# A Trainium2 trunk kernel: the state-space scans of half 0, two octets in one chain of operations

## The chip, the cores and the metric

The kernel runs on one core of one Trainium2 chip. The metric is device time in microseconds of one launch, as the median of several runs. Five engines work side by side, each on its own list of instructions in order: TensorE (PE: matmuls, into PSUM banks), VectorE (DVE), ScalarE (ACT), GpSimd (POOL) and SyncE (SP: here it only issues DMAs). They meet through semaphores. SBUF is the working memory; PSUM is the small memory that TensorE writes and that VectorE and ScalarE read and write.

## The reference, cut to what matters

One layer over 2048 positions of width 1024: a diagonal complex state-space mixer (S5), a gated linear unit behind it, a squared-ReLU MLP, a gated embedding and RMS norms. The change is in the mixer's scan:

```
bu_re = einsum('blgh,gph->blgp', ug, bb_re)      # 64 groups, 64 complex states each
bu_im = einsum('blgh,gph->blgp', ug, bb_im)
def combine(left, right):                        # x[l] = a * x[l-1] + bu[l], complex
    a1r, a1i, b1r, b1i = left
    a2r, a2i, b2r, b2i = right
    return (a2r*a1r - a2i*a1i, a2r*a1i + a2i*a1r,
            a2r*b1r - a2i*b1i + b2r, a2r*b1i + a2i*b1r + b2i)
_, _, xs_re, xs_im = associative_scan(combine, (a_re, a_im, bu_re, bu_im), axis=1)
y = einsum(xs_re, c_re) - einsum(xs_im, c_im)
```

## The kernel before, in words

The sequence is cut into two halves of 1024 positions, each half into 128 chunks of 8 positions. Inside a chunk the mixer is a product with small matrices that are made from powers of the decay; across the chunks a scan over 128 chunk states remains. The 64 groups form 8 octets of 8 groups; an octet's chunk states are a tile `xs` of 128 partitions (two groups' 64 states) by 2 (real, imaginary) by 4 by 128 chunks. The change concerns half 0, where octets are taken in four pairs (pair 0 to pair 3). Half 1 is scanned octet by octet later, from SBUF, between matmuls of the gated linear unit.

For an octet of half 0, `sums` (L595) has TensorE put the chunk sums into `xs`, a PSUM tile of its own from the pool `ps_x` with two buffers. `scan` (L613) then works on `xs` in place on VectorE: 7 levels up and 6 down, 13 in all, each with one multiplication by powers of the decay (`tm<-al,xs`) and two additions (`xs<-xs,tm`), every one dependent on the one before. `together` (L716) takes one operation of the pair's first octet, then one of its second, and so on, and starts other work of the plan at given steps. After that `stack` (L661) copies the result out of PSUM: on ScalarE, the first octet's copies and its `carry`, then the second's (in the last pair VectorE does the second's). Then TensorE makes the sums of the next pair's first octet, VectorE (or POOL) the matrices `vm` of that octet (`make_v`), then come the second octet's sums. The order on each engine is written out by hand there; the code order is the engine order. The low parts `al_y` of the mixer's output are made on VectorE inside the scans (`low`), after ScalarE has made the high parts `ah_y`.

At the start, `turned` (L244) turns the matrices b and c through TensorE into PSUM; four of its eight results use `ps_x` buffers, the other four other pools. In that part a scheduler sets the order on all engines but ScalarE. `al` (L124) holds the powers of the decay for all octets, `amul` (L618) forms a product with them, and the buffer `tm` (L854) has two copies in half 0.

Of the kernel before, what the change touches and what calls it, by code (L numbers as in the profile page):

```python
# [9 lines left out]
F32 = mybir.dt.float32  # L10
# [14 lines left out]
C = 128  # L25
# [5 lines left out]
NOCT = 8  # L31
# [7 lines left out]
def trunk(  # L39
# [31 lines left out]
    def tt(o, a, b, op):  # L71
        return dve.tensor_tensor(out=o, in0=a, in1=b, op=op)  # L72

    def mul(o, a, b):
        return tt(o, a, b, ALU.mult)
# [19 lines left out]
    const = ctx.enter_context(tc.tile_pool(name="const", bufs=1))  # L95
# [4 lines left out]
    ps_s5 = banks0.enter_context(tc.tile_pool(name="ps_s5", bufs=2, space=PSUM))  # L100

    sums0 = ExitStack()
    ps_x = sums0.enter_context(tc.tile_pool(name="ps_x", bufs=2, space=PSUM))
    ps_mm = None

    edge = ctx.enter_context(tc.tile_pool(name="edge", bufs=1, side="right"))
# [14 lines left out]

    ident = const.tile([P, P], F32, name="ident")
    make_identity(nc, ident)
    al = const.tile([P, 8, NOCT, 2, 2, 4], F32, name="al")  # L124
    carry = const.tile([P, 2, 32], F32, name="carry")
    dve.memset(carry, 0.0)
    g_ffn = const.tile([P, KT], F32, name="g_ffn")
# [85 lines left out]
    sp.dma_start(out=gn[:, 0], in_=norm_ffn[0].rearrange("(k q) -> k q", q=P))  # L213
    sp.dma_start(out=gn[:, 1], in_=norm_ple[0].rearrange("(k q) -> k q", q=P))
    xs0 = stat_loads(0)
    sq = small.tile([P, 2, NOCT, 4], F32, name="sq", bufs=1)
    sgn = sq[:, 0, 0, 0:1]
    pool.memset(sgn[0:S], 1.0)
    pool.memset(sgn[S:P], -1.0)
# [21 lines left out]
    y1 = par.tile([P, G, H], F32, name="y1")  # L241
    y2 = par.tile([P, G, H], F32, name="y2")

    def turned(above, below, hh, nm, pool_=None, tag="s5"):  # L244

        if pool_ is None:
            ps = ps_x.tile([P, 2, 8, G], F32, tag="x", name=f"bc_{nm}_{hh}")[:, 0]
        else:
            ps = pool_.tile([P, 8, G], F32, tag=tag, name=f"bc_{nm}_{hh}")
        for h in range(8):  # L250
            for half, src in enumerate((above, below)):
                if half:
                    pe.matmul(ps[S:P, h], src(hh * 8 + h), ident[0:G, 0:G], start=True, stop=True)  # L253
                else:
                    pe.transpose(out=ps[0:S, h], in_=src(hh * 8 + h), identity=ident[0:G, 0:G])
        return ps[:, :].rearrange("p h g -> p g h")
# [165 lines left out]

    for e in range(2):
        ls = slice(e * S, e * S + S)
        pr = pw_r[ls, 8].rearrange("p (o i e) -> p e o i", e=2, i=4)[:, e]
        pi = pw_i[ls, 8].rearrange("p (o i e) -> p e o i", e=2, i=4)[:, e]
        for r_ in range(2):
            dve.tensor_copy(out=al[ls, 0, :, 0, r_], in_=pr)
            ts(al[ls, 0, :, 1, r_], pi, 1.0 - 2 * r_, ALU.mult)

    def decay_steps():
        for k in range(7):
            re, im = al[:, k, :, 0, 0], al[:, k, :, 1, 0]
            mul(sq[:, 0], re, re)
            yield
            mul(sq[:, 1], im, im)
            yield
            ri = al[:, k + 1, :, 1, 1]
            mul(ri, re, im)
            yield  # L440
            tt(al[:, k + 1, :, 0], sq[:, 0].unsqueeze(2).broadcast_to([P, NOCT, 2, 4]),
               sq[:, 1].unsqueeze(2).broadcast_to([P, NOCT, 2, 4]), ALU.subtract)
            yield
            for r_ in range(2):
                ts(al[:, k + 1, :, 1, r_], ri, 2.0 - 4 * r_, ALU.mult)
                yield
# [18 lines left out]
    class Octet:  # L465
# [129 lines left out]
        def sums(self):  # L595

            if self.hb == 0:
                self.xs = ps_x.tile([P, 2, 4, C], F32, tag="x", name=f"xs_{self.nm}")
                for i in range(4):
                    for c in range(2):  # L600
                        for e in range(2):
                            pe.matmul(self.xs[e * S:(e + 1) * S, c, i], self.wm[:, 2 * i + e, c * S:(c + 1) * S],
                                      self.u[:, 2 * i + e], start=True, stop=True)
                return
            self.xs = self.tile("xs", (P, 2, 4, C))
            for e in range(2):
                ps = ps_s5.tile([P, 4, C], F32, tag="s5", name=f"s{e}_{self.nm}")
                for i in range(4):
                    pe.matmul(out=ps[:, i], lhsT=self.wm[:, 2 * i + e], rhs=self.u[:, 2 * i + e], start=True, stop=True)
                for c in range(2):  # L610
                    act.copy(self.xs[e * S:(e + 1) * S, c], ps[c * S:(c + 1) * S])

        def scan(self):  # L613

            xs, o, i0 = self.xs, self.o, 4 * self.o
            tm = self.tile("tm", (P, 16 * (C // 2)))

            def amul(k, src, n):  # L618
                t_ = tm[:, :16 * n].rearrange("p (a n) -> p a n", n=n)
                a_ = al[:, k, o].rearrange("p a r i -> p (a r i)").unsqueeze(2).broadcast_to([P, 16, n])  # L620
                s_ = src.rearrange("p r i c -> p (r i) c").unsqueeze(1).broadcast_to([P, 2, 8, n])
                mul(t_, a_, s_)
                t4 = tm[:, :16 * n].rearrange("p (a r i n) -> p a r i n", a=2, r=2, i=4)
                return t4[:, 0], t4[:, 1, ::-1]

            for k in range(6 if self.hb else 7):
                l = 1 << k
                t1, t2 = amul(k, xs[:, :, :, l - 1::2 * l], C // (2 * l))
                yield
                dst = xs[:, :, :, 2 * l - 1::2 * l]  # L630
                add(dst, dst, t1)
                yield
                add(dst, dst, t2)
                yield
            cr = carry[:, :, i0:i0 + 4].unsqueeze(3)
            if self.hb == 0:

                for k in range(5, -1, -1):
                    l = 1 << k
                    t1, t2 = amul(k, xs[:, :, :, 2 * l - 1:C - 1:2 * l], C // (2 * l) - 1)  # L640
                    yield
                    dst = xs[:, :, :, 3 * l - 1::2 * l]
                    add(dst, dst, t1)
                    yield
                    add(dst, dst, t2)
                    yield
                return
            self.es = es = self.tile("es", (P, 2, 4, C))
            e0 = es[:, :, :, 0:1]
            pool.tensor_copy(out=e0, in_=cr)  # L650
            for k in range(6, -1, -1):
                l = 1 << k
                t1, t2 = amul(k, es[:, :, :, 0::2 * l], C // (2 * l))
                yield
                dst = es[:, :, :, l::2 * l]
                add(dst, t1, xs[:, :, :, l - 1::2 * l])
                yield
                add(dst, dst, t2)
                yield
# [191 lines left out]

    EB = 3
    sp0 = s5.enter_context(tc.tile_pool(name="s5p", bufs=1, side="right"))
    nb0 = dict(u=4, vm=4, dd0=2, dd1=2, gm=3, tm=2)  # L854
    NP = NOCT // 2


# [24 lines left out]
    with tc.manual_schedule(engines=MANUAL):  # L882
# [94 lines left out]
        for k in range(NP):  # L977
            a, b = 2 * k, 2 * k + 1
            plan = PLAN0 if k == 0 else PLAN1 if k < NP - 1 else PLAN2
            at = [(n, lambda k=k, w=w, i=i: do(k, w, i)) for n, acts in plan for w, i in acts]  # L980
            together((q.scan() for q in pairs[k]), *at)
            octs[a].stack()
            octs[b].stack(k == NP - 1)
            if k < NP - 1:
# [603 lines left out]
```

## Time and profile before

| | |
|---|---|
| median of 3 runs | 2162.16 us (2161.92 to 2165.72) |
| the profiled execution | 2161.0 us, its span 2159.2 us |
| busy, share of the span | PE 94%, DVE 64%, ACT 41%, POOL 19% |
| the chain that ended last, by engine | PE 77%, DVE 12%, issue 3%, ACT 3%, POOL 3%, DMA 2% |
| mean granted TensorE clock | 0.984 |

Times in the rows are microseconds from the span's start. A timeline row merges like instructions that follow one another: start of the first, time from there to the end of the last, engine, line, operation, tile written <- tiles read, shapes, count; in brackets the idle time before it and what ended it. Operations overlap at their ends, so what an operation costs in a row of many is the distance between starts, not its own duration. DVE helpers all have one line (L72), so tiles tell which is which.

### The profile page before, as it was taken

To read this page: it belongs to the slowest core of one execution; us is meant where nothing else is said; L and a number is where in the kernel's file an instruction comes from. 1 tells how busy PE (TensorE), PEld (TensorE's weight loads), DVE (VectorE), ACT (ScalarE), POOL (GpSimd) and SP (SyncE) were. 2 spreads that over 40 slices of the span, in tenths; PEclk is the share of its full clock that TensorE was granted. 3 is DMA by queue.
4 is the path that set the end of the run, shared out by engine and by line. 5 is a ranking of instruction groups with operands and counts; after the bars stand their busy time and mean duration, and the time that the engine had idled before them with its cause. 6 is when DMAs were issued, how large, how long until landed. Compare 5 with 4: busy or idle time off the path is not lost.

```text
span 2159.2 us, 28823 instructions
## 1 busy us (share of the span) xinstructions
PE 2033.9 (94%) x9878; PEld 1680.1 (78%) x9878; DVE 1387.7 (64%) x2614; ACT 886.5 (41%) x1767; POOL 417.6 (19%) x369
## 2 busy tenths in 40 slices
PE   7488999987999999999999999979999999999997
PEld 5477877775788888888887788857888888888876
DVE  5998587766766666876665732367666657555455
ACT  2476354435333235444454521243323355444443
POOL 1575011112322221533210000022222200000000
PEclk9999999998999999999999999989999999999999
DMA  5297644342444449998861631224444498755112
GB/s 167 92 266 204 206 148 124 96 124 70 152 155 156 151 158 347 353 389 305 290 234 67 226 104 40 81 81 144 159 149 148 159 335 294 251 194 191 45 49 88
DMA packets 241957, 377.38 MB, mean 175 GB/s; under 512 B 23681, under 2 KB 106641, under 8 KB 241809
## 3 DMA queue, kind: packets, MB, share of 16 engines
q1 hardware_dynamic: 236880, 360.85, 49.9%
q0 software_dynamic: 4928, 14.69, 2.1%
q8 instruction: 77, 1.26, 0.2%
q14 instruction: 72, 0.58, 0.1%
HBM read 261.21 MB, written 114.23 MB: 174 GB/s over the span
## 4 chain that ended last, share of the span: by engine, by line
PE 77%; DVE 12%; issue 3%; ACT 3%; POOL 3%; DMA 2%; SPq 0%; DVEq 0%; ACTq 0%; POOLq 0%
PE dn L1358 28%; PE up L1266 26%; PE glu L1047 3%; PE glu L1049 3%; PE glu L1048 3%; PE gt L1049 2%; PE gt L1048 2%; PE gt L1047 2%; DVE tm L72 2%; DVE xs L72 2%; DVE es L72 1%; DVE wu L72 1%; ACT xs L668 1%; PE bc_b L253 1%; PE bc_c L253 1%
## 5 line engine op out<-in xcount | busy, mean ns | idle before, releaser
L1266 PE MATMUL up<-h_s,wu 128*128 128x512 f32 x1280 | 407.4, 392 | 6.9 <-DVE ev L72 6.9
L1358 PE MATMUL dn<-h_dw,h_da 128*128 128x512 f32 x896 | 349.1, 390 | 0.0
L1358 PE MATMUL dn<-h_dw,l_da 128*128 128x512 f32 x896 | 348.7, 389 | 0.0
L1358 PE MATMUL dn<-l_dw,h_da 128*128 128x512 f32 x896 | 348.6, 389 | 0.0
L1266 PEld LDWEIGHTS up<-h_s,wu 128*128 128x128 f32 x1280 | 242.4, 189 | 58.9 <-DVE ev L72 8.6
L72 DVE TENSOR_TENSOR l_da<-da,h_da 128x512 fp32r<-128x512 f32 x224 | 178.7, 798 | 168.7 <-ACT h_da L1174 168.6
L1266 PE MATMUL up<-l_s,wu 128*128 128x512 f32 x640 | 250.5, 391 | 0.0
L72 DVE TENSOR_TENSOR wu<-rawu,wu 128x512 fp32r<-128x512 f32 x224 | 164.2, 747 | 114.7 <-ACT wu L1254 114.7
L1174 ACT CAST h_da<-da 128x512 fp32r<-128x512 f32 x224 | 139.1, 621 | 235.8 <-PE dn L1358 211.2
L1047 PE MATMUL glu<-w_glu,ah_y 128*128 128x512 f32 x492 | 195.5, 397 | 5.6 <-ACT w_glu L734 4.7
L1358 PEld LDWEIGHTS dn<-h_dw,l_da 128*128 128x128 f32 x896 | 168.2, 188 | 34.9
L1358 PEld LDWEIGHTS dn<-h_dw,h_da 128*128 128x128 f32 x896 | 168.2, 188 | 34.8
L1358 PEld LDWEIGHTS dn<-l_dw,h_da 128*128 128x128 f32 x896 | 168.2, 188 | 34.7
L1048 PE MATMUL glu<-w_glu,ah_y 128*128 128x512 f32 x492 | 193.5, 394 | 1.3 <-DVE w_glu L72 1.3
L1049 PE MATMUL glu<-w_glu,al_y 128*128 128x512 f32 x492 | 192.6, 392 | 0.0
L1252 POOL TENSOR_TENSOR rawu<-rawu,rawu 128x512 f32<-128x512 f32 x96 | 134.7, 1417 | 298.1 <-DVE wu L72 298.1
L72 DVE TENSOR_TENSOR l_dw<-dw,h_dw 128x512 fp32r<-128x512 f32 x224 | 168.7, 753 | 12.4 <-ACT h_dw L1174 11.0
L1266 PE MATMUL up<-ah_f,wu 128*128 128x512 f32 x512 | 172.4, 398 | 3.5 <-ACT wu L1254 2.8
L1254 ACT CAST wu<-rawu 128x512 fp32r<-128x512 f32 x224 | 131.9, 620 | 91.0 <-POOL rawu L1252 62.2
L1174 ACT CAST h_dw<-dw 128x512 fp32r<-128x512 f32 x224 | 138.1, 617 | 46.1 <-POOL dw L1343 44.4
L1277 ACT COPY ev<-up 128x512 f32<-128x512 f32 x96 | 56.2, 585 | 245.2 <-PE up L1266 245.2
L1266 PEld LDWEIGHTS up<-l_s,wu 128*128 128x128 f32 x640 | 121.2, 189 | 25.2
(312 smaller groups left out, 3398.4 us busy)
## 6 DMA issues: line engine op xcount, KB each, us to landing
da<-h_d SPq DMA_DIRECT2D x224, 256.0 KB, 4.6
dw<-in_mlp_w_dram SPq DMA_DIRECT2D x192, 256.0 KB, 5.1
rawu<-in_mlp_w_dram SPq DMA_DIRECT2D x64, 512.0 KB, 3.8
h_d<-ev SPq DMA_DIRECT2D x96, 256.0 KB, 2.1
h_d<-hs SPq DMA_DIRECT2D x96, 256.0 KB, 2.1
dw<-t_d SPq DMA_DIRECT2D x96, 256.0 KB, 4.4
t_d<-dw SPq DMA_DIRECT2D x64, 256.0 KB, 5.1
raw_glu<-in_ssm_w_glu_dram SPq DMA_DIRECT2D x59, 256.0 KB, 4.0
```

What stands on the lines that cost most here:

```text
L72: return dve.tensor_tensor(out=o, in0=a, in1=b, op=op)
L253: pe.matmul(ps[S:P, h], src(hh * 8 + h), ident[0:G, 0:G], start=True, stop=True)
L668: act.copy(dd[c * S:(c + 1) * S, :, e], self.es[e * S:(e + 1) * S, c])
L1047: pe.matmul(out=ps, lhsT=lh, rhs=rh, start=first, stop=False)
L1048: pe.matmul(out=ps, lhsT=lh, rhs=rl, start=False, stop=False)
L1049: pe.matmul(out=ps, lhsT=ll, rhs=rh, start=False, stop=last)
L1174: act.copy(h_, src)
L1252: pool.tensor_tensor(out=src, in0=src, in1=other, op=ALU.add)
L1254: act.copy(w_[:, 0], src)
L1266: pe.matmul(out=ps, lhsT=lhs, rhs=rhs, start=i in FIRST_IN_CHAIN and k == n == 0, stop=k == 3 and n == 2, skip_group_check=True)
L1277: act.copy(ev[g, i], y_ if i == 5 else x_)
L1358: pe.matmul(out=ps, lhsT=lhs[:, cs_], rhs=rhs, start=i in FIRST_IN_CHAIN and fp == n == 0, stop=fp == NPAIR - 1 and n == 2, skip_group_che ...
```

## The change

In half 0 the sums of a pair's two octets share one PSUM tile of twice the size, `ps_x` has one buffer of that size, and one scan runs on both octets at once: each of its 39 operations is twice as wide, and there is one chain where there were two in turn. `al` is laid out by pairs of octets, so half 1's `amul` takes a slice of it. `turned` takes its four places from one `ps_x` tile. `tm` has one buffer of twice the size.

```
-    ps_x = sums0.enter_context(tc.tile_pool(name="ps_x", bufs=2, space=PSUM))
+    ps_x = sums0.enter_context(tc.tile_pool(name="ps_x", bufs=1, space=PSUM))
-    al = const.tile([P, 8, NOCT, 2, 2, 4], F32, name="al")
+    al = const.tile([P, 8, NOCT // 2, 2, 2, 8], F32, name="al")
...
         if pool_ is None:
-            ps = ps_x.tile([P, 2, 8, G], F32, tag="x", name=f"bc_{nm}_{hh}")[:, 0]
+            if not places:
+                four = ps_x.tile([P, 4, 8, G], F32, tag="x", name=f"bc_{nm}_{hh}")
+                places.extend(four[:, i] for i in range(4))
+            ps = places.pop(0)
...
             if self.hb == 0:
-                self.xs = ps_x.tile([P, 2, 4, C], F32, tag="x", name=f"xs_{self.nm}")
+                if self.o % 2 == 0:
+                    self.both = ps_x.tile([P, 2, 8, C], F32, tag="x", name=f"xs_{self.nm}")
+                else:
+                    self.both = octs[self.o - 1].both
+                self.xs = self.both[:, :, 4 * (self.o % 2):4 * (self.o % 2) + 4]
...
-            xs, o, i0 = self.xs, self.o, 4 * self.o
-            tm = self.tile("tm", (P, 16 * (C // 2)))
+            o, i0 = self.o, 4 * self.o
+            m = 4 if self.hb else 8
+            xs = self.xs if self.hb else self.both
+            tm = self.tile("tm", (P, 4 * m * (C // 2)))
             def amul(k, src, n):
...
+                if self.hb:
+                    a_ = al[:, k, o // 2, :, :, 4 * (o % 2):4 * (o % 2) + 4].unsqueeze(4).broadcast_to([P, 2, 2, m, n])
+                    mul(t_, a_, src.unsqueeze(1).broadcast_to([P, 2, 2, m, n]))
...
-    nb0 = dict(u=4, vm=4, dd0=2, dd1=2, gm=3, tm=2)
+    nb0 = dict(u=4, vm=4, dd0=2, dd1=2, gm=3)
...
-            together((q.scan() for q in pairs[k]), *at)
+            together([pairs[k][0].scan()], *at)
```

VectorE at the first scan (pair 0), before: `tm_0` and `xs_0` are the first octet's, `tm_1` and `xs_1` the second's.

```order
L72 TENSOR_TENSOR tm_0_833<-al,xs_0_730 128x1024 [waits PE_49]
L72 TENSOR_TENSOR tm_1_835<-al,xs_1_760 128x1024 [waits PE_49]
L72 TENSOR_TENSOR xs_0_730<-xs_0_730,tm_0_833 128x512 [waits DVE_49]
L72 TENSOR_TENSOR xs_1_760<-xs_1_760,tm_1_835 128x512 [waits DVE_49]
L72 TENSOR_TENSOR xs_0_730<-xs_0_730,tm_0_833 128x512 [waits DVE_49]
L72 TENSOR_TENSOR xs_1_760<-xs_1_760,tm_1_835 128x512 [waits DVE_49]
L72 TENSOR_TENSOR tm_0_833<-al,xs_0_730 128x512 [waits DVE_49]
L72 TENSOR_TENSOR tm_1_835<-al,xs_1_760 128x512 [waits DVE_49]
```

The same place now:

```order
L72 TENSOR_TENSOR tm_0_829<-al,xs_0_727 128x2048 [waits PE_49]
L72 TENSOR_TENSOR xs_0_727<-xs_0_727,tm_0_829 128x1024 [waits DVE_49] x2
L72 TENSOR_TENSOR tm_0_829<-al,xs_0_727 128x1024 [waits DVE_49]
L72 TENSOR_TENSOR xs_0_727<-xs_0_727,tm_0_829 128x512 [waits DVE_49] x2
L72 TENSOR_TENSOR tm_0_829<-al,xs_0_727 128x512 [waits DVE_49]
L72 TENSOR_TENSOR xs_0_727<-xs_0_727,tm_0_829 128x256 [waits DVE_49] x2
```

Two operations of different octets became one; each waits for the one right before it, where the other octet's operation stood between.

TensorE at the sums of pair 1, before: `xs_2` and `xs_3` are the two octets' tiles, `pp` the work before, `kp` the work behind.

```order
L812 MATMUL pp_1_1_0_1194<-plwh_0_583,plo_1_1_1045 128x512
L602 MATMUL xs_2_1202<-u_2_904,gm_2_603 64x128 [waits DVE_49,Activation_49]
L602 MATMUL xs_2_1202<-u_2_904,gm_2_603 64x128 x15
L602 MATMUL xs_3_1225<-u_3_1069,gm_3_823 64x128 [waits DVE_49,Activation_49]
L602 MATMUL xs_3_1225<-u_3_1069,gm_3_823 64x128 x15
L562 MATMUL kp_2_1260<-y_195,zz 32x16
```

The same place now:

```order
L827 MATMUL pp_1_1_0_1150<-plwh_0_580,plo_1_1_1024 128x512
L611 MATMUL xs_2_1158<-u_2_898,gm_2_600 64x128 [waits DVE_49,Activation_49]
L611 MATMUL xs_2_1158<-u_2_898,gm_2_600 64x128 x15
L611 MATMUL xs_2_1158<-u_3_1048,gm_3_819 64x128 x16
L567 MATMUL kp_2_1215<-y_195,zz 32x16
```

Both octets' sums now write one tile; the one wait left stands at its first matmul, and the second octet's matmuls carry none of their own.

TensorE in the parameter stage, before: `bc_c` are turned parts of c, `tp_small` four small transposes from which ScalarE makes `dm`.

```order
L255 MATMUL bc_c_1_476<-ident,cn_132 64x64
L253 MATMUL bc_c_1_476<-ident,cn_133 64x64
L255 MATMUL bc_c_1_494<-ident,cn_133 64x64
L381 MATMUL tp_small<-ident,dn 128x16
L382 MATMUL tp_small<-ident,dn 128x16
L383 MATMUL tp_small<-ident,gn 128x8
L384 MATMUL tp_small<-ident,gn 128x8
```

The same place now (the turned parts of c are in the tile that is named after b):

```order
L260 MATMUL bc_b_0_197<-ident,cn_132 64x64
L258 MATMUL bc_b_0_197<-ident,cn_133 64x64
L260 MATMUL bc_b_0_197<-ident,cn_132 64x64
L386 MATMUL tp_small<-ident,dn 128x16
L387 MATMUL tp_small<-ident,dn 128x16
L388 MATMUL tp_small<-ident,gn 128x8
L389 MATMUL tp_small<-ident,gn 128x8
```

The small transposes stand 8 matmuls (four steps of two) further ahead, at place 107 of TensorE's list and not at 115; as many matmuls of c follow them.

## Rows read from the trace of the kernel before

**Rows 1.** Windows: stretch, length, busy us (instructions) of PE, PEld, DVE, ACT, POOL; clock; DMA.

```profile
94.00:232.00 138.00, 121.90 (x1066) 104.97 (x1058) 124.82 (x364) 92.86 (x214) 71.98 (x67) 0.96 0.77 214
120.00:122.00 2.00, 1.95 (x18) 1.95 (x20) 1.97 (x2) 1.95 (x6) 2.00 (x2) 0.50 1.09 305
232.00:2159.00 1927.00, 1856.49 (x8512) 1536.76 (x8510) 1195.71 (x2057) 766.98 (x1489) 306.63 (x263) 0.99 0.51 174
```

**Rows 2.** Timeline, VectorE, scan of pair 2: start, duration, line, operation, count, [idle before].

```profile
158.69 2.34 DVE L72 TENSOR_TENSOR tm<-al,xs 128x1024 f32<-128x1024 f32 x2
160.95 2.48 DVE L72 TENSOR_TENSOR xs<-xs,tm 128x512 f32<-128x512 f32 x4
163.34 1.27 DVE L72 TENSOR_TENSOR tm<-al,xs 128x512 f32<-128x512 f32 x2
...
172.12 0.50 DVE L72 TENSOR_TENSOR xs<-xs,tm 128x8 f32<-128x8 f32 x4
172.53 0.30 DVE L72 TENSOR_TENSOR tm<-al,xs 128x16 f32<-128x16 f32 x2
```

**Rows 3.** Timeline, VectorE, the first scan of half 1: one chain of dependent operations.

```profile
261.98 1.23 DVE L72 TENSOR_TENSOR tm<-al,xs 128x1024 f32<-128x1024 f32 x1 [4.03 <-ACT xs L611]
263.25 1.42 DVE L72 TENSOR_TENSOR xs<-xs,tm 128x512 f32<-128x512 f32 x2
264.70 1.07 DVE L72 TENSOR_TENSOR tm<-al,xs 128x512 f32<-128x512 f32 x1
...
271.73 0.18 DVE L72 TENSOR_TENSOR es<-tm,xs 128x8 f32<-128x8 f32 x1
271.94 0.17 DVE L72 TENSOR_TENSOR es<-es,tm 128x8 f32<-128x8 f32 x1
```

**Rows 4.** Timeline, all engines, from the scan of pair 0 to that of pair 1.

```profile
117.27 1.16 ACT L676 COPY dd<-xs 64x508 f32<-64x508 f32 x2 [0.54 <-DVE xs L72]
117.73 1.43 DVE L521 TENSOR_TENSOR vm<-pw_r,y 128x1024 f32<-128x1024 f32 x1
...
120.05 5.19 PE L602 MATMUL xs<-u,gm 128*64 128x128 f32 x64 [2.68 <-ACT carry L677]
...
122.55 0.17 ACT L677 COPY carry<-xs 128x8 f32<-128x8 f32 x1
...
123.54 1.22 DVE L72 TENSOR_TENSOR tm<-al,xs 128x1024 f32<-128x1024 f32 x1
...
126.42 2.49 DVE L72 TENSOR_TENSOR xs<-xs,tm 128x512 f32<-128x512 f32 x4
```

**Rows 5.** Timeline, VectorE and TensorE, the hand-overs to pair 2 and pair 3.

```profile
149.74 3.57 DVE L521 TENSOR_TENSOR vm<-pw_r,y 128x1024 f32<-128x1024 f32 x1
...
155.15 1.97 PE L602 MATMUL xs<-u,gm 128*64 128x128 f32 x32 [0.75 <-ACT carry L677]
...
184.59 1.22 DVE L521 TENSOR_TENSOR vm<-pw_r,y 128x1024 f32<-128x1024 f32 x1
...
195.46 2.49 DVE L72 TENSOR_TENSOR xs<-xs,tm 128x512 f32<-128x512 f32 x4
```

**Rows 6.** Timeline, VectorE and TensorE: waits inside pairs 1 and 3.

```profile
146.17 1.29 DVE L72 TENSOR_TENSOR al_y<-tpy,ah_y 128x512 fp32r<-128x512 f32 x2 [0.74 <-ACT ah_y L741]
...
194.84 0.28 PE L564 MATMUL kp<-vm,zz 128*32 128x112 f32 x1 [0.88 <-POOL vm L524]
...
207.40 1.29 DVE L72 TENSOR_TENSOR al_y<-tpy,ah_y 128x512 fp32r<-128x512 f32 x2 [2.97 <-ACT ah_y L741]
...
214.01 1.29 DVE L72 TENSOR_TENSOR al_y<-tpy,ah_y 128x512 fp32r<-128x512 f32 x2 [3.40 <-ACT ah_y L741]
```

**Rows 7.** Timeline, VectorE and TensorE, the parameter stage at the start.

```profile
47.91 0.17 DVE L72 TENSOR_TENSOR dl<-dm 128x16 f32<-128x16 f32 x1 [14.26 <-ACT dm L388]
...
51.93 0.47 PE L253 MATMUL bc_c<-ident,cn 64*64 64x64 f32 x2
...
53.80 1.22 DVE L521 TENSOR_TENSOR gm<-pw_r,zz 128x1024 f32<-128x1024 f32 x1
```

More of the change, by code (lines that the diff above doesn't have):

```diff
@@ L215, in trunk @@
     xs0 = stat_loads(0)
-    sq = small.tile([P, 2, NOCT, 4], F32, name="sq", bufs=1)
+    sq = small.tile([P, 2, NOCT // 2, 8], F32, name="sq", bufs=1)
     sgn = sq[:, 0, 0, 0:1]
@@ L242, in trunk @@
     y2 = par.tile([P, G, H], F32, name="y2")
+    places = []
     def turned(above, below, hh, nm, pool_=None, tag="s5"):
         if pool_ is None:
-            ps = ps_x.tile([P, 2, 8, G], F32, tag="x", name=f"bc_{nm}_{hh}")[:, 0]
+            if not places:
+                four = ps_x.tile([P, 4, 8, G], F32, tag="x", name=f"bc_{nm}_{hh}")
+                places.extend(four[:, i] for i in range(4))
+            ps = places.pop(0)
         else:
@@ L424, in trunk @@
         ls = slice(e * S, e * S + S)
-        pr = pw_r[ls, 8].rearrange("p (o i e) -> p e o i", e=2, i=4)[:, e]
-        pi = pw_i[ls, 8].rearrange("p (o i e) -> p e o i", e=2, i=4)[:, e]
+        pr = pw_r[ls, 8].rearrange("p (o i e) -> p e o i", e=2, i=8)[:, e]
+        pi = pw_i[ls, 8].rearrange("p (o i e) -> p e o i", e=2, i=8)[:, e]
         for r_ in range(2):
@@ L440, in decay_steps @@
             yield
-            tt(al[:, k + 1, :, 0], sq[:, 0].unsqueeze(2).broadcast_to([P, NOCT, 2, 4]),
-               sq[:, 1].unsqueeze(2).broadcast_to([P, NOCT, 2, 4]), ALU.subtract)
+            tt(al[:, k + 1, :, 0], sq[:, 0].unsqueeze(2).broadcast_to([P, NOCT // 2, 2, 8]),
+               sq[:, 1].unsqueeze(2).broadcast_to([P, NOCT // 2, 2, 8]), ALU.subtract)
             yield
@@ L613, in scan @@
         def scan(self):
-            xs, o, i0 = self.xs, self.o, 4 * self.o
-            tm = self.tile("tm", (P, 16 * (C // 2)))
+            o, i0 = self.o, 4 * self.o
+            m = 4 if self.hb else 8
+            xs = self.xs if self.hb else self.both
+            tm = self.tile("tm", (P, 4 * m * (C // 2)))
             def amul(k, src, n):
[L619 to L624, printed above, removed]
+                t_ = tm[:, :4 * m * n].rearrange("p (a r i n) -> p a r i n", a=2, r=2, i=m)
+                if self.hb:
+                    a_ = al[:, k, o // 2, :, :, 4 * (o % 2):4 * (o % 2) + 4].unsqueeze(4).broadcast_to([P, 2, 2, m, n])
+                    mul(t_, a_, src.unsqueeze(1).broadcast_to([P, 2, 2, m, n]))
+                else:
+                    a_ = al[:, k, o // 2].rearrange("p a r i -> p (a r i)").unsqueeze(2).broadcast_to([P, 4 * m, n])
+                    s_ = src.rearrange("p r i c -> p (r i) c").unsqueeze(1).broadcast_to([P, 2, 2 * m, n])
+                    mul(tm[:, :4 * m * n].rearrange("p (a n) -> p a n", n=n), a_, s_)
+                return t_[:, 0], t_[:, 1, ::-1]
             for k in range(6 if self.hb else 7):
```

## The prediction

> **What bounds the kernel now.** I read the windows first, to see where TensorE idles. From 232 us to the end it is busy 1856 of 1927 us, so later stages go at its pace and hand on whatever start they get. From 94 to 232 us, where half 0 is scanned, it is busy 122 of 138 us and VectorE 125 of 138 [rows 1]: there VectorE's scans and their hand-overs decide. Then I read the scans operation by operation: what costs there is the distance from one start to the next [rows 2, 3]. Then the hand-overs from pair to pair (scan, copies on ScalarE, sums on TensorE, next scan), since the change puts both octets into one PSUM tile [rows 4, 5]; the waits that could swallow a delay [rows 6]; and the parameter stage, where the scheduler moved four transposes [rows 7].
>
> **The scan itself.** Per pair, 78 operations become 39 of twice the width. Two octets in turn: two products of 1024 columns start within 160.95 - 158.69 = 2.26 us, so 1.13 each; four additions of 512 take 163.34 - 160.95 = 2.39, so 0.60 each [rows 2]. That is 1.04 ns a column ((1130 - 598)/512) and 0.065 us fixed. Every operation waits for its own octet's last one, but the other octet's stands between and hides that wait. In half 1 there is one chain: the product of 1024 takes 263.25 - 261.98 = 1.27 to the next start, an addition of 512 (264.70 - 263.25)/2 = 0.725 [rows 3]: the same slope and 0.20 us fixed. So one chain pays 0.20 an operation where two chains pay twice 0.065: 0.07 more for each pair that is merged, in spite of half the count. For the smallest no pair costs less than such a chain either: two additions of 8 columns start within (172.53 - 172.12)/2 = 0.205, a chain needs 0.21 for one (271.94 - 271.73) [rows 2, 3], so merging changes 0.01 there. Summed over the 39 steps (25 wide ones by 0.07, 14 narrow ones by 0.01 to 0.05): 22.2 us a scan before by these two formulas, 24.3 after, +2.07. The bounds: if the chain's wait were hidden also in one chain, 39 operations at 0.065 fixed give 19.0, that is -3.2. Above, the waits on PSUM can't be much longer than half 1's in SBUF, since the narrow pairs show 0.205 from one addition to the next on the same sums; I take +2.07, as half 1's chain is the same code.
>
> A rule of the Trainium skill speaks for the change: VectorE: DVE Perf Modes, section Rules for kernel authors, says of chained operations to keep their count low, since each pays the emptying of the pipeline anyway and the semaphore adds nothing; its formula for an fp32 tensor_tensor has a fixed (151)/0.96 ns. By that, an estimate: 39 operations fewer save 6.1 us a scan. The trace does not agree for operations in turn: they start 0.065 us plus the columns apart.
>
> **The hand-over.** After a scan ScalarE copies both octets out, 5.45 us from its first copy to the second octet's carry (117.27 to 122.55 + 0.17). Before, the sums of the next pair's first octet waited for the first octet's carry alone, under VectorE's three operations for `vm`, which ended at 123.54 [rows 4]. Now one tile serves both: the only wait stands before the first matmul, and it must be the second octet's carry. The 64 matmuls of both sums then lie open: 5.19 us in rows 4, where TensorE had waited 2.68 us and its granted clock was 0.50, 1.2 GHz, at their start [rows 1]; in pair 2 32 of them took 1.97 us after a wait of 0.75 [rows 5]. TensorE now waits for another octet's copies, longer than those 2.68 us, so I take 5.2. The first product needs all of it, and takes 1.27 + 1.07 = 2.33 to the first addition. From the scan's end on VectorE (the start of `vm`) to the first additions: 0.1 to ScalarE's first copy, 5.45, 5.2, 0.05, 2.33 = 13.15 us. Before: 126.42 - 117.73 = 8.69; from 149.74 to the product at 158.69 and its additions at 160.95, 11.21; 195.46 - 184.59 = 10.87 [rows 2, 4, 5]. So +4.46, +1.95, +2.28: together +8.7. Behind VectorE waits only its own list, which is all of the stage; behind TensorE's wait stand `kp`, the outputs of the pair before and the gate products.
>
> **The start.** VectorE waits 14.26 us for `dm`, which comes from the moved transposes. Four steps of about 0.64 us earlier would be 2.6, but `gm` (53.80) lies in memory that the turning of c still reads until 51.93 + 0.47 = 52.40 [rows 7]. So it gains at most 53.80 - 52.4 - 0.1 = 1.3; I take -1.3, bounds 0 and -2.6.
>
> **Costed at nothing.** The `al` layout and half 1's sliced product have the same columns in the same operations; VectorE does them beside a busy TensorE. One `tm` buffer: its users are all on VectorE, in order. `ps_x` for the turned parts: they are read long before the first sums.
>
> **The sum.** VectorE reaches the additions of pair 3 later by -1.3 + 3 x 2.07 + 8.7 = +13.6, less the wait for `ah_y` in pair 1 that vanishes (0.74) [rows 6], +12.9. TensorE's sums of pair 3 come as late; behind them its 0.88 us wait for POOL's `vm` vanishes: +12.0. In the rest of pair 3 VectorE waits 2.97 and 3.40 us for `ah_y`, that is for TensorE and ScalarE [rows 6]; that covers its extra time there, and the fourth scan costs nothing more. The stage's end is TensorE's, +12.0, and the rest hands it on. Against the profiled execution's own 2161.0 us: 2173.0. The median shown, 2162.16, lies 1.2 above that execution; I leave the 1.2 in the range. Forecast 2173 us.
>
> **Rivals.**
> First, full clock: if the sums run at 1.97 us each in every hand-over, each is 1.3 us shorter, -3.9: 2169. For it: the later hand-overs run so now [rows 5]. Against it: their wait grows.
> Second, not slower: fewer operations pay off, because the wide chain runs at 0.065 us fixed. The scans then give -3.2 each: -1.3 - 9.6 + 8.7 = -2.2 on VectorE. TensorE, which still waits for the second carry, may be up to 4 us late all the same. Between the two: about 2162. It decides if the wide additions start under 1.14 us apart. For it: the count. Against it: half 1's chain [rows 3]. The rule of the Trainium skill above (VectorE: DVE Perf Modes, Rules for kernel authors) points the same way and further.
> Third, the delay is swallowed: VectorE's 6.4 us of waits in pair 3 [rows 6] show that the last pair isn't set by the scan; if only VectorE were late, 12.9 - 6.4 = 6.5 less what the sums' wait under `vm` leaves, about 2165. Against it: TensorE's own sums are what is late.
> Fourth, worse: the half clock lasts beyond the sums into the outputs behind them in each hand-over, as it takes 5.19 instead of 3.9 in the sums; another 1.3 each, 2177.
> Fifth, faster: the second with the start's whole 2.6 and no lateness of TensorE: 2157.
>
> **Chances and range.** The forecast's own case (2170 to 2175) 0.48, full clock 0.18, worse 0.12; those are slower, and with part of the third 0.80. Within 0.2% (4.3 us, about what a measurement of this kernel can tell from no change): the second and the rest of the third, 0.15. Faster: 0.05. The range takes in the full clock, the worse case and the third: 2164 to 2179.
>
> **What would show it.** VectorE: additions of 1024 columns of `xs` 1.25 to 1.27 us apart (right) or under 1.14 (second rival); a scan of pair 0 some 2 us longer with what stands between. TensorE: the 64 sums in one go behind the second `carry`, with a wait of over 5 us and a granted clock of half in the first 2 us; VectorE idle for up to 5 us before the first product of pair 1, which before came right after `vm` [rows 4]. `dm` some 2.6 us earlier and `gm` about 1.3. The gated unit's matmuls some 12 us later throughout. The forecast is wrong if the sums start behind the first octet's carry, or if TensorE is as far as before at 232 us all the same.

## The result and the profile after

The changed kernel takes 2184.79 us (median of four runs, 2182.99 to 2193.8), the kernel before 2163.94 in the same comparison: a ratio of 1.0106, 95% interval 1.009 to 1.0123. It is slower, as forecast, but by 20.9 us, where 2173 against 2162.16 was a forecast of 11, and it lies outside the range of 2164 to 2179. The profiled execution is the slowest of the four, 2193.8 us with a span of 2192.0; a second profile of the same kernel (first experiment) fell on the fastest of its five runs and has a span of 2176.8. The same waits stand in both; 15 us lie between them with nothing edited, so both are read below.

The windows of the profile after (columns as in [rows 1]) show that TensorE is busy 109.5 us of the 138 from 94 to 232, where it was busy 121.9 (the last scan of half 0 now ends only at 242.6), that it stands still ahead of the first hand-over's sums, and that its granted clock there is 0.50, the 1.2 GHz level:

```profile
94.00:232.00 138.00, 109.46 (x988) 95.99 (x988) 116.25 (x180) 89.10 (x203) 72.86 (x65) 0.90 0.68 189
128.00:130.00 2.00, 0.00 (x0) 0.00 (x0) 1.97 (x2) 1.95 (x5) 1.92 (x2) 0.50 0.85 336
130.00:132.00 2.00, 1.44 (x14) 1.44 (x16) 0.48 (x1) 1.99 (x7) 2.00 (x2) 0.50 0.38 152
```

**The scan** came as costed. The timeline of VectorE in the scan of pair 3 answers to [rows 2]:

```profile
213.02 2.29 DVE L72 TENSOR_TENSOR tm<-al,xs 128x2048 f32<-128x2048 f32 x1 [3.06 <-PE xs L611]
215.34 2.50 DVE L72 TENSOR_TENSOR xs<-xs,tm 128x1024 f32<-128x1024 f32 x2
217.88 1.22 DVE L72 TENSOR_TENSOR tm<-al,xs 128x1024 f32<-128x1024 f32 x1
...
227.91 0.40 DVE L72 TENSOR_TENSOR xs<-xs,tm 128x16 f32<-128x16 f32 x2
228.34 0.19 DVE L72 TENSOR_TENSOR tm<-al,xs 128x32 f32<-128x32 f32 x1
```

Two wide additions take 217.88 - 215.34 = 2.54 us, 1.27 each (forecast 1.25 to 1.27). The first step of the scan takes 217.88 - 213.02 = 4.86 us where it took 163.34 - 158.69 = 4.65 [rows 2], so three operations paid 0.07 each; two additions of 16 columns take 0.43 where four of 8 took 0.41.

**The hand-over** from pair 0 to pair 1, all three engines, answers to [rows 4]:

```profile
124.94 1.46 DVE L526 TENSOR_TENSOR vm<-pw_r,y 128x1024 f32<-128x1024 f32 x1
125.07 1.16 ACT L691 COPY dd<-xs 64x508 f32<-64x508 f32 x2 [1.97 <-DVE xs L72]
...
130.34 0.17 ACT L692 COPY carry<-xs 128x8 f32<-128x8 f32 x1
130.56 6.41 PE L611 MATMUL xs<-u,gm 128*64 128x128 f32 x64 [6.82 <-ACT carry L692]
...
137.02 2.29 DVE L72 TENSOR_TENSOR tm<-al,xs 128x2048 f32<-128x2048 f32 x1 [6.54 <-PE xs L611]
139.41 2.50 DVE L72 TENSOR_TENSOR xs<-xs,tm 128x1024 f32<-128x1024 f32 x2
```

The sums stand behind the second octet's carry, after a wait of 6.82 us, and VectorE waits 6.54 us for them. From the scan's end to the first additions pass 139.41 - 124.94 = 14.47 us, forecast 13.15 (its terms add up to 13.13), before 8.69. The two other hand-overs answer to [rows 5]:

```profile
163.23 1.98 DVE L526 TENSOR_TENSOR vm<-pw_r,y 128x1024 f32<-128x1024 f32 x1
...
177.27 1.23 DVE L72 TENSOR_TENSOR xs<-xs,tm 128x1024 f32<-128x1024 f32 x1
...
201.97 2.54 DVE L526 TENSOR_TENSOR vm<-pw_r,y 128x1024 f32<-128x1024 f32 x1
```

They take 177.27 - 163.23 = 14.04 and 215.34 - 201.97 = 13.37 us (11.21 and 10.87 before).

**The start** is where the forecast failed. The timeline of the parameter stage answers to [rows 7]:

```profile
45.68 0.17 DVE L72 TENSOR_TENSOR dl<-dm 128x16 f32<-128x16 f32 x1 [11.76 <-ACT dm L393]
...
52.53 0.69 ACT L408 ACTIVATE y<-bc_b,sq 128x512 f32<-128x512 f32 x1
53.27 0.31 PE L260 MATMUL bc_b<-ident,cn 64*64 64x64 f32 x1 [5.65 <-ACT y L408]
...
58.53 0.60 ACT L409 ACTIVATE y<-bc_b 128x512 f32<-128x512 f32 x1 [5.31 <-PE bc_b L258]
58.59 1.23 DVE L526 TENSOR_TENSOR gm<-pw_r,zz 128x1024 f32<-128x1024 f32 x1 [7.96 <-issue]
```

`dl` is 2.2 us earlier, where 2.6 was forecast. But TensorE's last turned table waits 5.65 us for ScalarE. Four of the turned tables now lie in one tile (its name, `bc_b`, stands for each of them): the program lets ScalarE read the third place before TensorE writes the fourth, and on this one tile the write stands behind that earlier read, though the places are different memory. ScalarE comes to that read only behind its squares of x and four other operations. `gm` follows at 58.59, +4.8 instead of -1.3.

**The last stack**, which was costed at nothing, shows a second wait of the same kind. Timeline of VectorE, ScalarE and TensorE from the waits for `ah_y` ([rows 6]) to the last pair's outputs and half 1's first product ([rows 3]):

```profile
226.49 1.29 DVE L72 TENSOR_TENSOR al_y<-tpy,ah_y 128x512 fp32r<-128x512 f32 x2 [1.57 <-ACT ah_y L756]
...
231.49 1.29 DVE L72 TENSOR_TENSOR al_y<-tpy,ah_y 128x512 fp32r<-128x512 f32 x2 [1.73 <-ACT ah_y L756]
...
242.64 0.16 DVE L687 COPY dd<-pw_i 128x4 f32<-128x4 f32 x1
...
245.54 1.37 DVE L687 COPY dd<-xs 64x508 f32<-64x508 f32 x2 [2.74 <-ACT carry L692]
...
248.85 0.77 PE L702 MATMUL y<-vm,dd 128*128 128x128 f32 x2 [3.12 <-DVE v_x L86]
...
286.13 1.23 DVE L72 TENSOR_TENSOR tm<-al,xs 128x1024 f32<-128x1024 f32 x1 [5.23 <-ACT xs L620]
```

In the last pair ScalarE copies the first octet and VectorE the second, side by side until now. VectorE waits 2.74 us for ScalarE's carry, as both read one tile. TensorE, which before was busy up to its outputs, waits 3.12 us for the copies (the row names an earlier VectorE operation) and starts the outputs at half clock (granted 0.50 over their first 2 us): 0.77 us for two matmuls that later take 0.39. The waits for `ah_y` shrank from 2.97 and 3.40 to 1.57 and 1.73, as forecast.

The Trainium skill (PSUM — Partial Sum Buffer, PSUM bank collisions raise a hardware error) tells that two engines may not use one bank and quadrant at once, reads against reads included; a bank is 2 KB a partition by the same page (Specifications (TRN2)). That does not ask for this wait: an octet's sums fill whole banks of that size (4 x 128 fp32), so the two octets never share one. The wait belongs to the tile, and the ninth experiment, with two tiles, does not have it. In the shared tile the two octets' banks alternate, so the run doesn't tell whether the wait goes by the whole tile or by the range that an octet spans in it; at the start the two places lie side by side, and TensorE waited all the same.

Where the time went, each stretch as it came minus before (VectorE's rows above and their counterparts; "after again" is the first experiment, "places first" the second). Two of the rows before that bound the stretches:

```profile
94.22 2.33 DVE L72 TENSOR_TENSOR tm<-al,xs 128x1024 f32<-128x1024 f32 x2
...
224.52 0.16 DVE L672 COPY dd<-pw_i 128x4 f32<-128x4 f32 x1
```

| stretch | forecast | after | after again | places first |
|---|---|---|---|---|
| up to the first product of scan 0 (before 94.22) | -1.3 | +5.65 | +2.70 | -3.09 |
| scan 0 (23.51) | +2.07 | +1.56 | +1.54 | +1.55 |
| scans 1 and 2 (46.96) | +3.40 | +1.56 | +0.88 | +0.87 |
| three hand-overs (30.77) | +8.7 | +11.11 | +9.19 | +9.25 |
| scan 3 (29.06) | -0.88 | -1.76 | -1.76 | -1.76 |
| last stack to half 1's first product (37.46) | 0 | +6.03 | +3.08 | +3.07 |
| from there to the end (1897.2) | 0 | +8.7 | +2.0 | +2.0 |
| sum | +12.0 | +32.8 | +17.6 | +11.9 |

The last stretch took 1896.7 to 1905.9 us over all profiles here, also with kernels that differ by little there (1904.0 in the third experiment, 1896.7 in the fourth), so 9 us of the first profile's 32.8 can't be put down to the change.

### The profile page after: what moved, and what is told of

It reads as the page before. It is cut to its first block, busy times and chain, and to the rows that moved or that the text cites. A ratio compares the mean times of both kernels' runs of the same rounds, so it can differ in the third digit from the quotient of the medians.

```text
span 2192.0 us, 28662 instructions
## 1 busy us (share of the span) xinstructions
PE 2046.2 (93%) x9878; PEld 1690.4 (77%) x9878; DVE 1385.1 (63%) x2458; ACT 887.7 (40%) x1767; POOL 421.1 (19%) x369
## 4 chain that ended last, share of the span: by engine, by line
PE 72%; DVE 16%; ACT 4%; issue 4%; DMA 2%; POOL 1%; SPq 0%; DVEq 0%; ACTq 0%; POOLq 0%
PE dn L1373 28%; PE up L1281 26%; DVE tm L72 3%; DVE xs L72 3%; PE glu L1062 3%; PE glu L1064 3%; PE glu L1063 3%; PE gt L1064 2%; PE gt L1062 2%; PE gt L1063 2%; DVE es L72 2%; DVE wu L72 1%; ACT xs L683 1%; PE bc_b L258 1%; DMA xl<-in_x_dram 1%
```

## The experiments

**The changed kernel again**, nothing edited.

> The changed kernel a second time, nothing edited. Its first profile had the first scan operation of half 1 at 286.1 us (before 262.0, +24.2) and the end at +32.8, while its other three times lay 20 to 23 us above before. Theory A (all of the loss is made before half 1 begins, the rest of the first profile is run variation): ratio 1.009 to 1.012, and a profile in which half 1's first scan operation is 23 to 25 us later than in before and the end as well, within 4 us. Rival (half 1 or the later stages lose too): the profile's end again 30 us or more above before's, with the growth after 300 us in the same stretch as in the first profile.

Measured: 2181.99 us (2178.65 to 2183.82), ratio 1.0085 (1.0071 to 1.01). Half 1 began 15.6 us later than before and the end came 17.6 later: theory A, that all is lost before half 1, but not its 23 to 25 us. The difference to the first profile begins ahead of the first scan. First profile, then this one; VectorE and GpSimd ahead of the first scan:

```profile
89.96 1.10 POOL L526 TENSOR_TENSOR gm<-pw_r,zz 128x512 f32<-128x512 f32 x1 [6.26 <-PE xs L611]
89.99 1.15 DVE L72 TENSOR_TENSOR al<-sq 128x64 f32<-128x64 f32 x1
...
99.87 2.27 DVE L72 TENSOR_TENSOR tm<-al,xs 128x2048 f32<-128x2048 f32 x1
```

```profile
89.96 0.22 DVE L72 TENSOR_TENSOR al<-sq 128x64 f32<-128x64 f32 x1
...
90.59 1.47 POOL L526 TENSOR_TENSOR gm<-pw_r,zz 128x512 f32<-128x512 f32 x1 [6.91 <-ACT xn L496]
...
96.92 2.27 DVE L72 TENSOR_TENSOR tm<-al,xs 128x2048 f32<-128x2048 f32 x1
```

Where GpSimd's product started 0.03 us ahead of VectorE's small one, that one took 1.15 instead of 0.22 us and ended when GpSimd's did; where GpSimd came 0.6 us later, GpSimd's took longer instead. VectorE's first product came 2.95 us earlier here. GpSimd started 0.16 to 0.17 us behind TensorE's first 32 sums in both profiles, and these took 2.41 us in the first and 3.06 in this one; why they did is open.

**All places first.** All tables of c are written before ScalarE reads the first:

```
+    c_turned = [[turned(c_of[i], c_of[1 - i], hh, f"c{i + 1}", *(() if hh else (ps_s5, "s5"))) for i in range(2)]
+                for hh in range(2)]
     for hh in range(2):
...
-        act.activation(y1[:, :, hs], turned(c_of[0], c_of[1], hh, "c1", ...), AF.Copy, scale=sgn)
+        act.activation(y1[:, :, hs], c_turned[hh][0], AF.Copy, scale=sgn)
...
```

> The changed kernel with all four turned tables written by TensorE before ScalarE reads the first of them, so that no write into a place of the shared tile stands behind a read of another place. Everything else as in the changed kernel. Theory A (the shared four-place tile cost the startup: gm came at 58.59 instead of 53.80, where -1.3 was forecast): gm at 52.5 to 53.5, first scan operation 5 to 6 us earlier than in the changed kernel, time 5 to 6.5 us below the changed kernel, ratio to before 1.007 to 1.008. Rival B (the startup's end is set by something else just behind, so the scan starts no earlier): within 1.5 us of the changed kernel, ratio 1.010.

Measured: 2172.82 us (2172.32 to 2180.16), ratio 1.0055 (1.0037 to 1.0072), 9 us under the changed kernel by medians and 5.7 by spans (2171.1, against 2176.8 of the fastest run above). Two of the six runs took 2178 and 2180 us. The row of `gm` and that of the first product of scan 0, VectorE:

```profile
52.80 1.22 DVE L528 TENSOR_TENSOR gm<-pw_r,zz 128x1024 f32<-128x1024 f32 x1 [2.20 <-issue]
...
91.13 2.27 DVE L72 TENSOR_TENSOR tm<-al,xs 128x2048 f32<-128x2048 f32 x1
```

Theory A: the wait on the shared tile is real and is paid to the end; by the medians the gain is more than its 5 to 6.5. Without the wait `gm` gains 1.0 us, about the -1.3 of the forecast, and the first product of scan 0 comes 3.1 us earlier than before.

**One tile at the start, in the kernel before.**

```
-    ps_x = sums0.enter_context(tc.tile_pool(name="ps_x", bufs=2, space=PSUM))
+    four0 = ExitStack()
+    ps_x = four0.enter_context(tc.tile_pool(name="ps_4", bufs=1, space=PSUM))
...
-            ps = ps_x.tile([P, 2, 8, G], F32, tag="x", name=f"bc_{nm}_{hh}")[:, 0]
+            if not places:
+                four = ps_x.tile([P, 4, 8, G], F32, tag="x", name=f"bc_{nm}_{hh}")
+                places.extend(four[:, i] for i in range(4))
+            ps = places.pop(0)
```

> The kernel before with only the startup's four-place tile of the change; scans, sums and pairs as before. Theory A: the same wait of TensorE for ScalarE's read, gm 5 to 6 us later than before (53.80) or 5 less what the earlier dm gives (1.3), so +4 to +6 us: 2166 to 2168, ratio 1.002 to 1.0028. Rival B (the wait is there, but hidden): 2161 to 2163, ratio 0.999 to 1.0005. Rival C (the loss at the start belongs to the wider table al, not to the tile): no wait before bc_b's last place, and no loss.

Measured: 2168.91 us (2164.66 to 2173.33), ratio 1.0024 (1.0011 to 1.0036). TensorE and VectorE:

```profile
53.22 0.31 PE L261 MATMUL bc_b<-ident,cn 64*64 64x64 f32 x1 [5.67 <-ACT y L409]
...
58.51 1.23 DVE L529 TENSOR_TENSOR gm<-pw_r,zz 128x1024 f32<-128x1024 f32 x1 [7.95 <-issue]
```

Theory A: `gm` came at 58.51 behind a TensorE wait of 5.67 us for ScalarE's `y`, and `al` kept its layout, which rules out C. Alone, this part of the change costs 4.7 us.

**Copies in the other order, in the kernel before.**

```
+            if k < NP - 1:
+                octs[b].stack()
+                octs[a].stack()
+            else:
...
```

> The kernel before with the copies of the two octets of pairs 0 to 2 in the other order: the octet whose buffer the next pair's sums take first is copied last, so TensorE's sums start behind both copies as in the change, while tiles, scans and startup stay. Theory A (half of the loss is the hand-over: the sums behind the second copy, and at half clock): each of three hand-overs grows by the second copy and carry, 2.5 to 3.5 us, less than the 4.5, 2 and 2.3 predicted for the change only where one octet's 32 sums can start the scan: in all +6 to +10 us, 2168 to 2172, ratio 1.003 to 1.0046. Rival B (the hand-over is hidden by other work on VectorE, and the wide chain costs it all): +0 to +2 us, ratio under 1.001.

Measured: 2164.32 us, ratio 1.0001 (0.999 to 1.0011). The number is rival B's, but the edit did not do what it was for. The sums began behind the first of the two carries all the same (wait 3.24 us, 2.68 before): the pool hands out the buffer that comes free first, whichever octet had it. It tells nothing of the hand-over; the next one does.

**Both carries last, in the kernel before.**

```
-            octs[a].stack()
-            octs[b].stack(k == NP - 1)
+            octs[a].stack(hold=k < NP - 1)
+            octs[b].stack(k == NP - 1, hold=k < NP - 1)
+            if k < NP - 1:
+                octs[a].keep_carry()
+                octs[b].keep_carry()
```

> The kernel before, pairs 0 to 2: both octets' stacks are copied first and the two copies of the carry come last, so that both buffers come free only behind all ten copies, as in the change; tiles, two chains and startup stay. (Swapping the two stacks did not do this: TensorE still took the buffer that came free first, its sums began 0.8 us later.) Theory A (the hand-over of one shared tile costs what the prediction gave it, 8.7 us less the waits it swallows): sums 2.5 to 3 us later behind each of three scans, first additions 2.5 to 4 us later behind scan 0 and 1.5 to 2.5 behind scans 1 and 2, time +5 to +8 us, 2169 to 2172, ratio 1.0025 to 1.004. Rival B (the time between two scans is filled by other work of VectorE, and only the wide chain costs): +0 to +2 us, ratio under 1.001.

Measured: 2169.61 us (2167.08 to 2174.69), ratio 1.003 (1.0019 to 1.0041). The first hand-over, TensorE and VectorE:

```profile
117.94 1.21 DVE L521 TENSOR_TENSOR vm<-pw_r,y 128x1024 f32<-128x1024 f32 x1
...
123.02 5.07 PE L602 MATMUL xs<-u,gm 128*64 128x128 f32 x64 [5.43 <-ACT carry L682]
...
126.39 1.22 DVE L72 TENSOR_TENSOR tm<-al,xs 128x1024 f32<-128x1024 f32 x1 [2.99 <-PE xs L602]
...
129.28 1.29 DVE L72 TENSOR_TENSOR xs<-xs,tm 128x512 f32<-128x512 f32 x2
```

Theory A: the sums start 123.02 - 120.05 = 3.0 us later and the additions come 11.34 us behind the scan (8.69 before). At the two later hand-overs they come 11.5 and 13.1 us behind the scan (11.21 and 10.87 before), at the first of these with less than theory A's delay. The late release alone costs 5.9 us; what is left to the change, by its rows, is that the first product needs all 64 sums and is twice as wide: its first hand-over takes 13.2 to 14.5 instead of 11.3.

**Transposes in TensorE's waits**, on the kernel with all places first.

```
+                warm = ps_tp.tile([P, 4, C], F32, tag="tp", name=f"warm_{k}")
+                for i in range((44, 32, 27)[k]):
+                    pe.transpose(out=warm[:, i % 4], in_=ident[:], identity=ident[:])
                 octs[a + 2].sums()
```

> The changed kernel without the startup's wait (as in the run with all places first), and with 44, 32 and 27 transposes of the identity on TensorE, whose results nobody reads, in its waits before the sums of pairs 1 to 3, so that it does not stand still there. Theory A (the wait itself costs TensorE its clock: the 64 sums take 5.2 to 5.4 us behind the wait, and would take 3.9 at 1.97 per 32): sums in 3.9 to 4.1 us, first products 1.2 to 1.5 us earlier, three times, 3 to 5 us below the run with all places first, ratio to before 1.003 to 1.0045. Rival B (TensorE is back at full clock soon enough that the scan's start doesn't notice, or the transposes delay the sums by as much): within 1.5 us of the run with all places first.

Measured: 2187.03 us (2182.28 to 2188.56), ratio 1.0104 (1.0085 to 1.0122), 14 us above its base: neither theory. The transposes' tile had to wait for its buffer in the second and third hand-over, 6.9 us for VectorE's `al_y`, and pushed the sums back. The third, TensorE:

```profile
207.24 5.12 PE L1007 MATMUL warm<-ident 128*128 128x128 f32 x27 [6.93 <-DVE al_y L72]
212.29 3.71 PE L613 MATMUL xs<-u,gm 128*64 128x128 f32 x64
```

As a time it is a failure; as a trace it shows the sums in 3.71 us where they come right behind other matmuls. In the first hand-over, 2.03 us of standing still were left and the sums took 5.38. Their row, and the windows of the standing still and of the first 2 us of the sums (columns as in [rows 1]):

```profile
124.92 5.38 PE L613 MATMUL xs<-u,gm 128*64 128x128 f32 x64 [2.03 <-ACT carry L694]
```

```profile
122.90:124.90 2.00, 0.00 (x0) 0.00 (x0) 1.97 (x2) 1.95 (x6) 2.00 (x2) 1.00 0.95 389
124.90:126.90 2.00, 1.98 (x28) 1.98 (x30) 0.67 (x1) 2.00 (x7) 1.17 (x3) 0.76 0.82 320
```

**The fourth early product in the last wait**, on the kernel with all places first.

```
-    EB = 3
+    EB = 4
```

> The changed kernel without the startup's wait, and with the fourth early product (15 matmuls, 3.4 us) ahead of the last pair's outputs instead of behind them: it fills the 3.1 us that TensorE waits there for the copies of the last stack. Theory A (the last stack, costed at nothing in the prediction, costs the wait of 3.1 us and the half clock behind it, 8.8 us of output matmuls instead of 7.1): 3 to 5 us below the run with all places first, ratio to before 1.003 to 1.0045. Rival B (what follows waits for the outputs and ScalarE's activations, not for TensorE): within 1.5 us of it. Rival C: later than it by up to 1 us, as the outputs start behind the product.

Measured: 2174.02 us (2171.89 to 2180.73), ratio 1.0044 (1.0027 to 1.0061), against 1.0055 of its base: by the times rival B or too small to tell. The outputs now run at full clock (0.38 us for the first two), and from scan 3's end to half 1's first product pass 275.48 - 236.39 = 39.1 us instead of 40.5. So the trace returns 1.4 of the last stack's 3.1, not theory A's 3 to 5.

**Four tiles at the start, in the kernel before.**

```
-    ps_x = sums0.enter_context(tc.tile_pool(name="ps_x", bufs=2, space=PSUM))
+    start0 = ExitStack()
+    ps_x = start0.enter_context(tc.tile_pool(name="ps_4", bufs=4, space=PSUM))
...
-            ps = ps_x.tile([P, 2, 8, G], F32, tag="x", name=f"bc_{nm}_{hh}")[:, 0]
+            ps = ps_x.tile([P, 8, G], F32, tag="x", name=f"bc_{nm}_{hh}")
```

> The kernel before with four tiles of one bank each, from a pool of their own, for the startup's turned tables: no write waits for a read of another table, and no table waits for a buffer. Theory A (this is what the prediction's -1.3 us was for: dl and dm earlier by 2.2, gm by 1.3): gm at 52.5 to 53, time 0.5 to 1.5 us below before, ratio 0.9993 to 0.9998, within what can be told from no change. Rival B: gm no earlier, no change. Rival C: later, if TensorE's new order pushes another table back.

Measured: 2166.74 us (2163.59 to 2171.44), ratio 1.0019 (1.0009 to 1.003): rival C. With no table waiting for a buffer the scheduler put the four small transposes behind all four tables, TensorE and VectorE:

```profile
52.36 0.28 PE L382 MATMUL tp_small<-ident,dn 16*128 16x16 f32 x1
...
53.34 0.17 DVE L72 TENSOR_TENSOR dl<-dm 128x16 f32<-128x16 f32 x1 [19.13 <-ACT dm L389]
...
59.22 1.23 DVE L524 TENSOR_TENSOR gm<-pw_r,zz 128x1024 f32<-128x1024 f32 x1
```

The last table ends at 52.4 here and in the kernel before; what counts is the place of those four transposes ahead of it (46.92 before, 44.67 with all places first).

**The last pair apart**, on the kernel with all places first: pair 3 gets two tiles, two chains and two stacks again.

```
+                self.apart = self.o >= NOCT - 2
+                if self.apart:
+                    self.xs = ps_last[0].tile([P, 2, 4, C], F32, tag="x", name=f"xs_{self.nm}")
...
-            together([pairs[k][0].scan()], *at)
+            together([q.scan() for q in pairs[k][:1 if k < NP - 1 else 2]], *at)
...
+                if k == NP - 2:
+                    first.close()
+                    ps_last.append(sums0.enter_context(tc.tile_pool(name="ps_last", bufs=2, space=PSUM)))
```

> The changed kernel without the startup's wait, with its last pair alone as in the kernel before: two tiles, two chains, two stacks (their products in two buffers of the weights' pool); pairs 0 to 2 stay wide. Theory A (one shared tile makes VectorE's copies wait for ScalarE's): VectorE's copies start right behind the scan (2.7 us earlier), scan 3 takes up to 1.8 us more since its waits for ah_y come back, from scan 3's end to half 1's first scan operation 37.5 to 38 us instead of 40.5; time 1 to 3 us below the run with all places first. Rival B (the wait is for something else than the shared tile): VectorE's copies still wait 2.7 us, 40.5 us to half 1, no gain.

Measured: 2178.75 us (2172.87 to 2181.16), ratio 1.0062 (1.0046 to 1.0078), its base 1.0055. VectorE:

```profile
235.90 0.16 DVE L698 COPY dd<-pw_i 128x4 f32<-128x4 f32 x1
236.02 1.37 DVE L698 COPY dd<-xs 64x508 f32<-64x508 f32 x2
...
273.62 1.23 DVE L72 TENSOR_TENSOR tm<-al,xs 128x1024 f32<-128x1024 f32 x1 [4.03 <-ACT xs L627]
```

VectorE's copies no longer wait, and half 1 follows after 37.7 us: theory A's mechanism. Its gain in time is not there: scan 3 took 235.90 - 206.17 = 29.7 us instead of 27.3, more than the 1.8 us of the expectation, and the last stretch to the end took 1904.3 us where its base's profile has 1899.2, within the spread named above.

**One scan behind the other, in the kernel before.**

```
-            together((q.scan() for q in pairs[k]), *at)
+            together([one_by_one(pairs[k])], *((2 * n - 1, f) for n, f in at))
```

> The kernel before with the two scans of a pair one behind the other instead of interleaved (same operations, same widths, the plan's places at twice the count), so that each operation needs the one just ahead of it. Theory A (an operation that needs the one ahead of it costs 0.135 us more than one that doesn't, the rule by which the wide chain was costed): 78 operations by 0.135 is 10.5 us a scan, less what inserted operations cover, 7 to 10 us in each of scans 0 to 2, with the fourth in all +22 to +38 us, ratio 1.010 to 1.0175. Rival B (cost goes by the count of operations, whatever needs what): within 2 us of before. The hand-over keeps its place in the program.

Measured: 2188.15 us (2184.4 to 2190.8), ratio 1.0109 (1.0094 to 1.0125). Scan 0, from its first product at 94.27 to `vm` at 126.85, took 32.58 us instead of 23.51: +9.1, in theory A's 7 to 10, as is the whole time in its 22 to 38 (+25.0). The two rows, VectorE:

```profile
94.27 1.21 DVE L72 TENSOR_TENSOR tm<-al,xs 128x1024 f32<-128x1024 f32 x1
...
126.85 2.07 DVE L521 TENSOR_TENSOR vm<-pw_r,y 128x1024 f32<-128x1024 f32 x1
```

The same operations at the same widths cost 0.12 us more each where each needs the one ahead of it.

**The start with all places first, in the kernel before**: the one-tile start, with the edit of the second experiment.

> The kernel before with the startup of the run with all places first: one four-place tile, all four tables written before ScalarE's first read, which also puts the four small transposes (dn, gn) ahead of the last two tables on TensorE. Pairs, scans and stacks as before. Theory A: gm at 52.8 instead of 53.80 and the first scan operation 1 to 3 us earlier than 94.22, time 1 to 3 us below before, ratio 0.9985 to 0.9996. Rival B (what the start gains is lost again at the first hand-over or in the planner's order): ratio 0.9995 to 1.0005.

Measured: 2164.55 us (2159.01 to 2170.58), ratio 1.0005 (0.9993 to 1.0017). In the trace the first product came at 91.73 and half 1 began 2.1 us earlier (259.86), but the span is 2159.2 as before. By the times this is rival B; no gain can be told. This was the one version that might have beaten both kernels.

**More transposes, one hand-over**: 62 ahead of pair 1's sums only, one run of 2174.72 us.

> The changed kernel without the startup's wait, with 62 transposes that nobody reads ahead of the sums of pair 1 alone. With 44 of them TensorE stood still for 2.0 us behind them and the sums still took 5.38 us; where it had transposes until the sums began, 56 sums took 3.28. Theory A (TensorE's clock falls with the wait, and sums right behind work run at full clock): the wait ahead of the sums is 0 to 0.3 us and the 64 sums take 3.8 to 4.0. Rival B (the sums are slow for another reason, say the banks that they write): 5.2 to 5.4 us again.

TensorE, and the window of the sums (columns as in [rows 1]):

```profile
117.85 6.93 PE L1008 MATMUL warm<-ident 128*128 128x128 f32 x62
124.85 3.71 PE L613 MATMUL xs<-u,gm 128*64 128x128 f32 x64
```

```profile
124.80:128.60 3.80, 3.75 (x74) 3.58 (x78) 0.00 (x0) 3.80 (x13) 3.78 (x6) 1.00 0.75 292
```

Theory A: with no wait ahead of them the sums run at a granted clock of 1.00 (2.4 GHz) in 3.71 us instead of 5.2 to 6.4, and the hand-over takes 131.00 - 119.21 = 11.8 us instead of 13.3.

## Why the prediction was wrong in size

**The step that failed is the start**, "I take -1.3", with bounds of 0 and -2.6. It measured +4.8 at `gm`, a swing of 6.1, and +2.7 to +5.65 at the first product of scan 0. The term rested on when the memory of `gm` comes free, and that reading held: with all places first `gm` starts at 52.80, 0.1 us behind the last turned table. But it did not ask what the new, common tile makes wait for what. "`ps_x` for the turned parts: they are read long before the first sums" looked at the next user of the tile, not at its own four writers and readers. Putting the writes first took 5.7 us (spans) to 9 us (medians) off the changed kernel, and the tile alone put 4.7 us on the kernel before. Without this fault the change takes 2172.8 us, where 2173 was forecast, but that agreement is partly luck: in its trace the last stack and the stretch behind it add 5.1 us that the forecast had at nothing, and the start and the scans came 5.7 us cheaper than forecast.

**"Costed at nothing": the last stack.** It is the same oversight, two engines on one tile: +3.1 us in the trace, 2.7 of it VectorE's wait. Taking the wait away by two tiles brought the stretch back to 37.7 us; how much of it reaches the time is open, since neither experiment on it lowered the median (2174.0 and 2178.75 us against 2172.8).

**The scan, +2.07 each**, is right by the operation (0.07 a merged pair in the first steps, 0.02 in narrow ones; a whole scan of operations that each need the one ahead costs 0.12 each by the tenth experiment, where the forecast's fixed costs of 0.20 and 0.065 differ by 0.135) and too large as a stretch: +1.55 in scan 0, and +0.9 (+1.6 in the slowest profile) for scans 1 and 2 together with the vanished wait, where +3.4 was forecast. My reading, not tested by itself, is that other operations inserted between two links fill the gap that a single chain leaves. The rule of the Trainium skill named in the forecast (VectorE: DVE Perf Modes, Rules for kernel authors) did not decide here: half the count made scan 0 1.55 us longer, not 6.1 shorter. The rule is for chained operations, and before, the operation ahead was in general the other octet's.

**The hand-overs, +8.7,** measured +9.2 in two profiles and +11.1 in the slowest. Terms: the wait for the second carry as forecast; the 64 sums 5.2 to 5.4 us in the quieter profiles (5.2 forecast) and 6.41, 6.05 and 5.38 in the slowest, where the granted clock over the first two was 0.57 and 0.60 (0.71 and 0.68 in the first experiment). The rivals on the clock were about this alone, 1.5 us a hand-over.

**Scan 3 and `ah_y`**: as forecast, VectorE's waits covered the longer chain; the stretch came out 1.76 us shorter than before, where 0.88 was forecast.

**The range** ended at 2179 because every rival varied terms that I had written down. None of them was a further wait by tile.

## What to carry over

When several buffers become one tile, list all its writers and readers in the order of the program, on every engine: here a write waited for an earlier read of another place in the tile, and a reader on one engine for a reader on another. Emit all writes ahead of the first read, or keep separate tiles. Merging two interleaved chains into one wide chain halves the count but takes away the work that hid each link's delay; count the distance from start to start, not instructions.

## What the runs showed of the hardware

- TensorE's clock is lost by short waits, and the loss can show only when the wait is over: in the sixth experiment the granted clock was still 1.00 over 2.0 us of standing still and 0.76 over the first 2 us of the sums, and 64 of them took 5.38 us; right behind other matmuls they took 3.71 at 1.00.
- A GpSimd product that starts just ahead of a small VectorE operation holds it for its own length: 0.22 became 1.15 us. With GpSimd 0.6 us later the first scan began 2.95 us earlier. The Trainium skill (SBUF — State Buffer, SBUF: two separate sides) describes an exclusive lock between the two; the rows agree.
- An identical kernel began half 1 at 286.1 and at 277.6 us in two profiles, so a single profile doesn't tell the size of an effect under 10 us in this stage.
